# A hybrid encoder layer on one core: gates and keys made beside the input projection, and the scan's blocks in another order

## The chip, the core and the metric

The kernel runs on 1 core of one Trainium2 chip. Five engines work at the same time, each on its own queue of instructions: TensorE (PE, with its weight loads PEld), VectorE (DVE), ScalarE (ACT), GpSimd (POOL) and SyncE (SP, which here only issues DMAs). An instruction waits at the head of its queue until what it needs is there, and everything behind it waits too. The metric is the device time of one execution in microseconds (us); less is better.

## The reference

One layer of an encoder over 1024 positions of 1024 features, in float32, with one projection that feeds two mixers:

```python
proj = jnp.einsum("bsd,de->bse", h, w_in)          # h = rmsnorm(x)
glu_in, q, v, z_f, z_b, og, g_a, g_b = jnp.split(proj, SPLIT_POINTS, axis=-1)
a = jax.nn.glu(glu_in, axis=-1)
a = _dwconv_centred(a, dw_w, dw_b)                 # 31 taps, 512 channels
a = jax.nn.silu(_layernorm(a, ln_w, ln_b))
a = jnp.einsum("bsc,cd->bsd", a, pw_w)
o = _bi_hgrn2(q, v, z_f, z_b, lb[0], lb[1])        # 8 heads of 128, two directions
```

In `_bi_hgrn2` each direction turns its z into a forget gate and a key:

```python
f = lb + (1.0 - lb) * jax.nn.sigmoid(zf)
lf = jnp.log(jnp.clip(f, MIN_FORGET, 1.0))
key_gate = (1.0 - lb) * jax.nn.sigmoid(-zf)
```

and a gated linear recurrence runs over the positions with state `S_t = diag(f_t) S_{t-1} + k_t v_t^T` and output `S_t^T q_t`. Then come a norm by head times `silu(og)`, an output matrix, the merge `sigmoid(g_a) * a + sigmoid(g_b) * b`, `w_out` with the residual, a convolutional GLU feed-forward block, and a last RMSNorm.

## The kernel before

**Matmuls.** A float32 operand is split into two parts (`split`, L125: ACT rounds the high part, another engine subtracts), and `mm3` (L149 to L151) makes three matmuls of 128x128 by 128x512 for each k. TensorE gets its instructions in the order in which the program writes them; the other engines' order is set by a planner, except for instructions marked with `pin`, which keep the program's order among themselves. The work is written as streams of pieces: a piece is six such matmuls, and `Stream.fill(n)` lets n pieces be written at that place, fractions being carried over.

**Input pairs** (`pair_job`, `in_pair`). Two column tiles of `w_in` are made together by seven products in place of eight. The products run in the order 1, 2, 6, 7, 5, 4, 3, two pieces each, so a pair has 14 pieces. ACT copies three of them to SBUF pages (`su`, L440), and four evacuations (`evac`) follow, after products 2, 5, 4 and 3: three of them a DVE sum or difference of a product and an `su` page (`ev`, L800), the last straight from PSUM. 19 pairs make 38 of 56 tiles: q and og of each head, then v, z forward and z backward of each head but the last. The last head's two z tiles and the 16 tiles of g_a and g_b are made later as ordinary jobs (`rest_jobs`). The sums of weights that a pair needs are made by accumulating DMAs from GpSimd's queue (L302), or, with `first`, by DVE (L298): so for pair 0 and pairs 14 to 18. `store` (L796 to L806) evacuates a tile to an `ev` page (three of them) and stores it to DRAM through SP's queue; z is stored raw.

**Convolution and norm beside the pairs.** The 124 steps of the depthwise convolution (L1036, L1039, on DVE, four channel tiles in the pages `gl`) are written between pieces of pairs, `CONV_FILL` = 1.67 pieces a step. Then comes the LayerNorm of two halves: load, mean by a matmul with ones (L1065), squares, a reciprocal root (two small GpSimd operations, L592 and L593, then four ACT copies and a matmul, L600 and L601), and for each of four channel tiles two DVE operations, Silu on ACT (L1079), a split and two stores. The fills there are 6, 6 and 5 pieces, and 12 (`LN_LAST`) after all four tiles.

**The scan** (L1150 to L1480). 16 blocks: 8 heads by two halves of 512 positions. For block i the inputs are loaded (`scan_inputs`: q, both z; ACT makes two sigmoids and f of each z, L1163 to L1165; DVE clamps f, L1166), two blocks ahead. `scan_base` then works in five steps: it scales the keys (L1224), and doubles the span of keys `kG` and queries `qF` from 1 to 32 by DVE products (L1144), with woven copies on ACT (L1176); step 3 issues a level of 128 small matmuls (128x32, L1195, into a bank `sc`). `scan_levels` issues, with a break after each: the levels 8 and 16 (64 matmuls, L1195, into `ob`); the zeroing of a bank by 16 matmuls (`none`, L1302), the 32 blocks of span 32 (L1281) and the doubling by 32; the 16 blocks of span 64 (L1281, shape 128x64) and the doubling by 64. Four transposes of v (L1470) come after the second of these breaks has begun. `scan_states` transposes the keys (L1320), breaks, multiplies them with v (L1329), and breaks. In each of the five breaks a block writes 1.77 pieces (`FILL`) of dense jobs, one step of the next block's base, and one step of the outputs (`scan_outputs`) of the head before. Of the outputs, two steps hold 22 matmuls each (L1370) and two hold four transposes each (L1396).

**The end.** The last product of the feed-forward block runs in three parts (512, 256 and 256 positions). Each result is added (L1879) and, four pieces later, turned by transposes (`turn_out`, L1890), squared on ACT (L1892), multiplied by the final gain (L1905) and scaled by the row's factor (`scale_out`: DVE for 640 columns, L1928, ACT for the rest, L1926).

Of the kernel before, what the change touches and what calls it, by code (L numbers as in the profile page):

```python
# [15 lines left out]
ALU = mybir.AluOpType  # L16
# [4 lines left out]
TAIL = ((1, 2), (1, 1), (2, 4), (2, 3))  # L21
CONV_FILL = 1.67
NPAIRS = 19
LN_FILL = 6
LN_LAST = 12
GLU_FIRST = 4
# [3 lines left out]
GLU_LATE = 17  # L30
BASE_STEPS = 1
ALIGN = 128
# [16 lines left out]
def tile_hybrid_encoder(  # L49
# [45 lines left out]
    def nm(s):  # L95
        uid[0] += 1
        return f"{s}_{uid[0]}"
# [58 lines left out]

    chores = []

# [4 lines left out]
    def advance_chores(n=1):  # L163
        for c in list(chores):
            c[0] -= n
            if c[0] <= 0:
                chores.remove(c)
                c[1]()

    class Weights:  # L170
# [393 lines left out]
    d_og = scratch("d_og", NH, 2)  # L564
    d_z = scratch("d_z", 2, NH, 2)
    d_bm = scratch("d_bm", NH, 2)
# [229 lines left out]
    def store(dst, func=None):  # L796
# [11 lines left out]
        return evac  # L808

    todo = [  # L810
        t
# [5 lines left out]
    ]  # L817
    todo += [
        t
        for h in range(NH)  # L820
        for t in (
            (OFF_V + h * DK, store(d_v[h])),
            (OFF_ZF + h * DK, store(d_z[0][h])),
            (OFF_ZB + h * DK, store(d_z[1][h])),
        )
    ]
    todo += [(OFF_GA + i * P, store(d_ga[i], AF.Sigmoid)) for i in range(ND)]
    todo += [(OFF_GB + i * P, store(d_gb[i], AF.Sigmoid)) for i in range(ND)]

    def in_pair(n):  # L830
        (c0, e0), (c1, e1) = todo[2 * n], todo[2 * n + 1]
        evs = (e0, e1)
        return pair_job(
            in_cols(c0),
            in_cols(c1),
            NK2,
            lambda i: ht[i],
            p1,
            p1,
            lambda e, *quadrant: evs[e](*quadrant),  # L840
            first=n == 0 or n >= 14,
            columns=2,
        )
# [145 lines left out]
    V.tensor_scalar(lbw[:, 3, :], lbw[:, 2, :], -1.0, 1.0, op0=ALU.mult, op1=ALU.add)  # L989

    def lb_of(d, h):
        return lbw[:, 2, d * NH + h : d * NH + h + 1]
# [63 lines left out]
    for half in range(2):  # L1056
        xs = []
        for j in range(NCW):
            if j % 2 == 0:
                both = p1.tile([P, 2, H], F32, tag="ca", name=nm("cx"), bufs=2)  # L1060
            nc.sync.dma_start(both[:, j % 2, :], d_cv[j][half])
            xs.append(both[:, j % 2, :])
        s_pairs.fill(LN_FILL)
        mean = bank("ob")
        T.matmul(mean, ones_m, total(xs, tmp()), start=True, stop=True)  # L1065
        for t in xs:
            V.scalar_tensor_tensor(t, mean, -1.0 / CW, t, op0=ALU.mult, op1=ALU.add)
# [7 lines left out]
        rs = next(rstd)  # L1075
        for j, xn in enumerate(xs):
# [68 lines left out]

    kscale = cp.tile([P, 2 * NH], F32, name="kscale")
    V.tensor_scalar(kscale, lbw[:, 3, :], DK**-0.5, None, op0=ALU.mult)

    def c4(t):
        return t.rearrange("p (c t) -> p c t", c=4)  # L1150

    def scan_inputs(i):
# [7 lines left out]
        for d in range(2):  # L1160
            z = page(hp, "zi", 3)
            nc.sync.dma_start(z, d_z[d][h][half])
            A.activation(kG[:, d, :], z, AF.Sigmoid, scale=-1.0)  # L1163
            A.activation(z, z, AF.Sigmoid)
            A.activation(f[:, d, :], z, AF.Identity, scale=oml_of(d, h), bias=lb_of(d, h))  # L1165
        V.tensor_scalar(f, f, MIN_FORGET, 1.0, op0=ALU.max, op1=ALU.min)  # L1166
        return q, f, kG, kscale[:, h : h + NH + 1 : NH]

# [48 lines left out]
    def scan_base(ins):  # L1217


        q, f, kG, ks = ins  # L1220
        qF = hp.tile([P, 2, H], F32, tag="qF", name=nm("qF"), bufs=4)
        D_t = hp.tile([P, 4, 32], F32, tag="D", name=nm("D"), bufs=3)
        for d in range(2):
            V.tensor_scalar(kG[:, d, :], kG[:, d, :], ks[:, d : d + 1], None, op0=ALU.mult)  # L1224
        k_d, Q1 = page(hp, "A", 8), page(hp, "A", 8)
# [44 lines left out]
    def scan_levels(base, S_t, Tt):  # L1270
# [24 lines left out]
        level(slot(b, 0), A8, row(Q8))  # L1295
        level(slot(b, 1), A16, row(Q16))
        for n, m in enumerate((m_8, m_16)):
            V.copy_predicated(D_t, over(m), near(slot(b, n)))
        yield
        b = bank("sc")  # L1300
        for at, g, _ in each():
            T.matmul(b[g, at : at + 32], none, none, start=True, stop=True)  # L1302
# [137 lines left out]
    cur = Base(scan_inputs(0))  # L1440
    ins = scan_inputs(1)
    dense.fill(7)
    for pieces in (3, 4, 4, 3, 0):
        cur.step(1)
        dense.fill(pieces)
    pending = Stream(iter(()))
    for h in range(NH):
# [4 lines left out]
        for half in range(2):  # L1452
            i = 2 * h + half
            base = cur.result()
            ahead = Base(ins) if i + 1 < NI else None
            ins = scan_inputs(i + 2) if i + 2 < NI else None

            def between(fill):
                dense.fill(fill)
                if ahead is not None:  # L1460
                    ahead.step(BASE_STEPS)
                pending.fill(1)

            S_t = hp.tile([P, 4, P], F32, tag="S", name=nm("S"), bufs=3)
            vl = load(d_v[h][half])
            for n, _ in enumerate(scan_levels(base, S_t, Tt[:, half])):
                if n == 1:
# [4 lines left out]
                    A.copy(v.rearrange("p c e -> p (c e)"), b)  # L1472
                between(FILL)
            qF, kG = base[:2]
            for _ in scan_states(i, kG, v, Tt, Sf, Sb):
                between(FILL)
            kept.append((S_t, v, qF))
            cur = ahead
        pending = Stream(outputs(h, kept, Tt, Sf, Sb))
# [560 lines left out]
```

## Time and profile before

| | us |
|---|---|
| median of 3 runs | 1736.81 |
| lowest and highest run | 1735.74 and 1737.69 |
| the profiled execution's own time | 1736.41 |
| its span, from the first to the last instruction | 1734.3 |
| DMA moved | 308.27 MB, mean 178 GB/s |

The mean granted TensorE clock was 0.998. The profile counts an engine as busy from the start of an instruction to its end. Matmuls overlap, so PE's busy time says little about how densely it runs; the distance from one start to the next, or the number of matmuls in a stretch, does. In rows of groups the last field is the engine's idle time just before them and what ended it. In rows of waits the three numbers are the total in us, the count and the longest.

### The profile page before, as it was taken

The page shows a single profiled execution, that of the slowest core. Times are in us where ns is not written, and L with a number is a line of the kernel's source. Part 1 is how long each engine was busy: PE and PEld are TensorE (multiplying, and loading weights), DVE is VectorE, ACT ScalarE, POOL GpSimd, SP SyncE. Part 2 cuts the span into 40 slices and gives each one's busy share as a digit, 9 for nine tenths or more (in the row PEclk, how much of TensorE's full clock was granted, in tenths as well). Part 3 has the DMA queues.
Part 4 walks back from the last instruction along what each step waited for, and adds up shares of the span by engine and source line. Part 5 has one row for each costly group of instructions (what it writes and reads, how often), then busy time and mean ns, then how long its engine had stood idle before and what let it go on. Part 6 is the DMA issues. An engine that isn't in the chain of part 4 may idle for free.

```text
span 1734.3 us, 30669 instructions
## 1 busy us (share of the span) xinstructions
PE 1709.2 (99%) x11902; PEld 1415.0 (82%) x11902; DVE 1255.9 (72%) x1937; ACT 830.3 (48%) x1544; POOL 170.4 (10%) x185
## 2 busy tenths in 40 slices
PE   8999999999999999999999999999999999999997
PEld 6878888888788888888878888888888888888787
DVE  5599999746778888888557466667767776657865
ACT  7444443334566777776442245444434433542334
POOL 2211111100000000000000002011111111000110
PEclk9999999999999999999999999999999999999999
DMA  8768888854673444435579466568777776783842
GB/s 288 239 167 184 193 194 193 197 167 154 207 230 104 131 126 132 127 115 192 175 248 333 147 207 205 146 148 170 158 170 160 180 172 153 229 267 107 205 91 98
DMA packets 343751, 308.27 MB, mean 178 GB/s; under 512 B 25262, under 2 KB 255798, under 8 KB 343606
## 3 DMA queue, kind: packets, MB, share of 16 engines
q1 hardware_dynamic: 289590, 267.51, 48.7%
q0 software_dynamic: 44800, 37.76, 15.2%
q10 hardware_dynamic: 9216, 1.05, 0.4%
q8 instruction: 93, 1.52, 0.4%
q14 instruction: 52, 0.43, 0.1%
HBM read 201.40 MB, written 87.03 MB: 166 GB/s over the span
## 4 chain that ended last, share of the span: by engine, by line
PE 44%; DMA 2%; DVE 2%; ACT 1%; issue 1%; SPq 0%; POOL 0%; POOLq 0%; ACTq 0%; DVEq 0%
PE mm L151 10%; PE mm L150 10%; PE mm L149 10%; PE sc L149 3%; PE sc L150 3%; PE sc L151 3%; PE tr L149 1%; PE tr L150 1%; PE tr L151 1%; DMA tm<-d_bm 1%; DVE hx L125 0%; DMA wr<-in_ffn_w_down_dram 0%; DMA wr<-wr 0%; DMA d_gc<-ft 0%; DVE wp L125 0%
## 5 line engine op out<-in xcount | busy, mean ns | idle before, releaser
L149 PE MATMUL mm<-hx,wp 128*128 128x512 f32 x1068 | 428.0, 401 | 3.3 <-ACT tm L851 2.1
L151 PE MATMUL mm<-hx,wp 128*128 128x512 f32 x1068 | 418.1, 391 | 0.9 <-DVE wp L125 0.8
L150 PE MATMUL mm<-hx,wp 128*128 128x512 f32 x1068 | 416.9, 390 | 0.3 <-DVE hx L125 0.2
L125 ACT CAST wp<-wr 128x1024 fp32r<-128x1024 f32 (+2 forms) x147 | 147.2, 1002 | 259.2 <-PE mm L150 119.5
L151 PEld LDWEIGHTS mm<-hx,wp 128*128 128x128 f32 x1068 | 200.9, 188 | 46.3 <-DVE wp L125 3.4
L149 PEld LDWEIGHTS mm<-hx,wp 128*128 128x128 f32 x1068 | 200.8, 188 | 46.1 <-ACT tm L851 2.6
L150 PEld LDWEIGHTS mm<-hx,wp 128*128 128x128 f32 x1068 | 201.2, 188 | 41.3 <-DVE hx L125 1.6
L125 DVE TENSOR_TENSOR wp<-wr,wp 128x1024 fp32r<-128x1024 f32 (+2 forms) x145 | 169.3, 1168 | 68.5 <-ACT wp L125 67.9
L1039 DVE SCALAR_TENSOR_TENSOR acc<-gl,v_b,acc 128x1024 f32<-128x1024 f32 x120 | 148.9, 1277 | 0.4
L1144 DVE TENSOR_TENSOR qF<-qF,tb 128x512 f32<-128x512 f32 x96 | 65.0, 684 | 20.8 <-ACT A L1176 20.7
L440 ACT COPY su<-mm 128x512 f32<-128x512 f32 x82 | 47.7, 582 | 66.2 <-PE mm L151 66.2
L149 PE MATMUL tr<-hx,wp 128*128 128x512 f32 x180 | 70.5, 392 | 0.0
L125 ACT CAST wq<-sw 128x1024 fp32r<-128x1024 f32 x41 | 43.2, 1053 | 56.3 <-PE mm L150 40.5
L151 PE MATMUL tr<-hx,wp 128*128 128x512 f32 x180 | 70.1, 389 | 0.0
L150 PE MATMUL tr<-hx,wp 128*128 128x512 f32 x180 | 70.0, 389 | 0.0
L1636 DVE SCALAR_TENSOR_TENSOR tm<-gp,v_a,tm 128x512 f32<-128x512 f32 x88 | 65.9, 749 | 3.9 <-ACT tm L1634 2.0
L1144 DVE TENSOR_TENSOR kG<-kG,tb 128x512 f32<-128x512 f32 x96 | 65.1, 684 | 3.7 <-PE sc L1281 3.7
L149 PE MATMUL mm<-hy,wp 128*128 128x512 f32 x164 | 64.2, 391 | 0.0
L149 PE MATMUL sc<-hy,wq 128*128 128x512 f32 x164 | 64.2, 391 | 0.0
L151 PE MATMUL sc<-hy,wq 128*128 128x512 f32 x164 | 63.8, 389 | 0.0
L150 PE MATMUL mm<-hy,wp 128*128 128x512 f32 x164 | 63.8, 389 | 0.0
L150 PE MATMUL sc<-hy,wq 128*128 128x512 f32 x164 | 63.8, 389 | 0.0
(372 smaller groups left out, 3609.9 us busy)
## 6 DMA issues: line engine op xcount, KB each, us to landing
wr<-in_w_in_dram SPq DMA_DIRECT2D x48, 512.0 KB
wr<-in_ffn_w_up_dram SPq DMA_DIRECT2D x22, 512.0 KB
sw<-in_w_in_dram SPq DMA_DIRECT2D x38, 256.0 KB
d_g<-ft SPq DMA_DIRECT2D x38, 256.0 KB
sw<-in_ffn_w_up_dram SPq DMA_DIRECT2D x38, 256.0 KB
sw<-in_ffn_w_up_dram POOLq DMA_DIRECT2D x19, 512.0 KB, 8.1
wr<-sw POOLq DMA_DIRECT2D x32, 256.0 KB, 3.8
wr<-wr POOLq DMA_DIRECT2D x32, 256.0 KB, 4.1
```

Of the source, the lines that this page charges most:

```text
L125: parts = A.copy(hi, src), eng.tensor_tensor(lo, src, hi.bitcast(F32), op=ALU.subtract)
L149: T.matmul(acc, whi[:, k, :], ahi, start=first, stop=False, skip_group_check=again)
L150: T.matmul(acc, whi[:, k, :], alo, start=False, stop=False, skip_group_check=again)
L151: T.matmul(acc, wlo[:, k, :], ahi, start=False, stop=last, skip_group_check=again)
L440: A.copy(t, acc)
L1039: V.scalar_tensor_tensor(acc, g[:, k : k + S], tap(k), acc, op0=ALU.mult, op1=ALU.add)
L1144: V.tensor_tensor(o, a, b, op=op)
L1636: V.scalar_tensor_tensor(c, g[:, o + k : o + k + H], vec("fdw", k * NF + j), c, op0=ALU.mult, op1=ALU.add,)
```

## The change

Three things. **Gates and keys:** `store_gates` replaces the raw store of z. At each of the next three pieces one step runs: the complement's sigmoid into a key page (`complement`), the gate's sigmoid and the key's scale (`forget`), the affine bound (`bound`); two pieces later the clamp. Gate and key are stored through GpSimd's queue. The tiles are dealt in another order (q and og, six v, gates of heads 0 to 6, the last two v), and pairs 12 and 13 too make their weight sums on DVE. The scan loads gates and keys ready made. **Norm:** Silu becomes a sigmoid on ACT and a product on DVE, with 1.5 pieces between the two and after each tile; other fills are 9 for the first, and 1.6 for a step of the convolution. **Scan and end:** levels 8 and 16, zeroing and the 32-blocks are one group with no break between them; a break with only v's transposes follows; then the 64-blocks. The first step of a base moves to the last break of the block before last, and in a break the outputs' step comes ahead of the base's. At the end, parts of 256 turn out six pieces late and scalings are six pieces apart.

```diff
-CONV_FILL = 1.67
+CONV_FILL = 1.6
-LN_LAST = 12
+LN_STEP = 1.5
-BASE_STEPS = 1
...
+    chores, paced = [], collections.deque()
...
     def advance_chores(n=1):
...
+        if paced:
+            paced.popleft()()
...
+    def gl_page():
+        return gp0.tile([P, 2, H], F32, tag="gl", name=nm("kp"), bufs=NCW)[:, 0, :]
+
+    def store_gates(d, h, key_page):
+        def evac(half, x0, x1=None, op=None):
+            f, x, key = ev(), x0, []
+            if x1 is not None:
+                V.tensor_tensor(f, x0, x1, op=op)
+                x = f
+
+            def complement():
+                key.append(key_page())
+                pin(A.activation(key[0], x, AF.Sigmoid, scale=-1.0))
+
+            def forget():
+                pin(A.activation(f, x, AF.Sigmoid))
+                if h == 0:
+                    pin(A.activation(key[0], key[0], AF.Copy, scale=kscale_of(d, h)))
+                else:
+                    pin(V.tensor_scalar(key[0], key[0], kscale_of(d, h), None, op0=ALU.mult))
+
+            def bound():
+                pin(A.activation(f, f, AF.Identity, scale=oml_of(d, h), bias=lb_of(d, h)))
+                later(1, lambda: G.dma_start(d_k[d][h][half], key[0]))
+                later(2, clamp)
+
+            def clamp():
+                eng = G if h == 0 else V
+                pin(eng.tensor_scalar(f, f, MIN_FORGET, 1.0, op0=ALU.max, op1=ALU.min))
+                later(1, lambda: G.dma_start(d_f[d][h][half], f))
+
+            paced.extend((complement, forget, bound))
+
+        return evac
...
-    todo += [
-        t
+    values = [(OFF_V + h * DK, store(d_v[h])) for h in range(NH)]
+    gate_tiles = [
+        (off + h * DK, store_gates(d, h, gl_page if 0 < h < NPAIRS - 12 else tmp))
         for h in range(NH)
-        for t in (
-            (OFF_V + h * DK, store(d_v[h])),
-            (OFF_ZF + h * DK, store(d_z[0][h])),
-            (OFF_ZB + h * DK, store(d_z[1][h])),
-        )
+        for d, off in enumerate((OFF_ZF, OFF_ZB))
     ]
+    n = 2 * (NPAIRS - 12)
+    todo += values[:-2] + gate_tiles[:n] + values[-2:] + gate_tiles[n:]
...
-            first=n == 0 or n >= 14,
+            first=n == 0 or n >= 12,
...
-        s_pairs.fill(LN_FILL)
+        s_pairs.fill(LN_FILL + 3)
...
-            A.activation(xn, xn, AF.Silu)
-            both = gp0.tile([P, 2, H], F32R, tag="gl", name=nm("ch"), bufs=NCW)
-            for dst, part in zip(d_ca[j][half], split(both[:, 0, :], both[:, 1, :], xn, V)):
-                nc.sync.dma_start(dst, part.bitcast(F32))
-        s_pairs.fill(LN_LAST)
+            sig = tmp()
+            A.activation(sig, xn, AF.Sigmoid)
+            s_pairs.fill(LN_STEP)
+            V.tensor_tensor(xn, xn, sig, op=ALU.mult)
+            store_parts(j)
+            s_pairs.fill(LN_STEP)
...
         for d in range(2):
-            z = page(hp, "zi", 3)
-            nc.sync.dma_start(z, d_z[d][h][half])
-            A.activation(kG[:, d, :], z, AF.Sigmoid, scale=-1.0)
-            A.activation(z, z, AF.Sigmoid)
-            A.activation(f[:, d, :], z, AF.Identity, scale=oml_of(d, h), bias=lb_of(d, h))
-        V.tensor_scalar(f, f, MIN_FORGET, 1.0, op0=ALU.max, op1=ALU.min)
-        return q, f, kG, kscale[:, h : h + NH + 1 : NH]
+            nc.sync.dma_start(f[:, d, :], d_f[d][h][half])
+            nc.sync.dma_start(kG[:, d, :], d_k[d][h][half])
+        return q, f, kG
...
-        for d in range(2):
-            V.tensor_scalar(kG[:, d, :], kG[:, d, :], ks[:, d : d + 1], None, op0=ALU.mult)
...
         level(slot(b, 1), A16, row(Q16))
+        S_b = bank("sc")
+        for at, g, _ in each():
+            T.matmul(S_b[g, at : at + 32], none, none, start=True, stop=True)
+        blocks(S_b, 32)
         for n, m in enumerate((m_8, m_16)):
             V.copy_predicated(D_t, over(m), near(slot(b, n)))
-        yield
-        b = bank("sc")
-        for at, g, _ in each():
-            T.matmul(b[g, at : at + 32], none, none, start=True, stop=True)
-        blocks(b, 32)
         tb = double(tb, 32)
         yield
+        yield
+        b = S_b
         blocks(b, 64)
...
-    ins = scan_inputs(1)
+    ahead = Base(scan_inputs(1))
...
+    ahead.step(1)
...
-            def between(fill):
-                dense.fill(fill)
-                if ahead is not None:
-                    ahead.step(BASE_STEPS)
+            following = Base(scan_inputs(i + 2)) if i + 2 < NI else None
+
+            def between(n):
+                dense.fill(FILL)
                 pending.fill(1)
+                step_of = ahead if n < 4 else following
+                if step_of is not None:
+                    step_of.step(1)
...
-            cur = ahead
+            cur, ahead = ahead, following
...
-        later(4, lambda: turn_out(i, half, chunks))
+        later(8 - len(chunks), lambda: turn_out(i, half, chunks))
...
-        st.fill(4 * ND * (n + 1) + 3 - st.count)
-        finish(*part, late=2 + 2 * n)
+        st.fill(4 * ND * (n + 1) + (3, 5)[n] - st.count)
+        finish(*part, late=6)
```

`store_parts` is the split and the two stores that stood in the loop; `kscale` is now made ahead of the pairs.

More of the change, by code (lines that the diff above doesn't have):

```diff
@@ L153, in tile_hybrid_encoder @@
     PRODUCTS = (1, 2, 6, 7, 5, 4, 3)
-    chores = []
+    chores, paced = [], collections.deque()
     def later(n, do):
@@ L564, in tile_hybrid_encoder @@
     d_og = scratch("d_og", NH, 2)
-    d_z = scratch("d_z", 2, NH, 2)
+    d_f = scratch("d_f", 2, NH, 2)
+    d_k = scratch("d_k", 2, NH, 2)
     d_bm = scratch("d_bm", NH, 2)
@@ L989, in tile_hybrid_encoder, with kscale_of @@
     V.tensor_scalar(lbw[:, 3, :], lbw[:, 2, :], -1.0, 1.0, op0=ALU.mult, op1=ALU.add)
+    kscale = cp.tile([P, 2 * NH], F32, name="kscale")
+    V.tensor_scalar(kscale, lbw[:, 3, :], DK**-0.5, None, op0=ALU.mult)
+    def kscale_of(d, h):
+        return kscale[:, d * NH + h : d * NH + h + 1]
     def lb_of(d, h):
@@ L1075, in tile_hybrid_encoder, with store_parts @@
         rs = next(rstd)
+        def store_parts(j):
+            both = gp0.tile([P, 2, H], F32R, tag="gl", name=nm("ch"), bufs=NCW)
+            for dst, part in zip(d_ca[j][half], split(both[:, 0, :], both[:, 1, :], xs[j], V)):
+                nc.sync.dma_start(dst, part.bitcast(F32))
         for j, xn in enumerate(xs):
@@ L1144, in tt @@
         V.tensor_tensor(o, a, b, op=op)
-    kscale = cp.tile([P, 2 * NH], F32, name="kscale")
-    V.tensor_scalar(kscale, lbw[:, 3, :], DK**-0.5, None, op0=ALU.mult)
     def c4(t):
@@ L1217, in scan_base @@
     def scan_base(ins):
-        q, f, kG, ks = ins
+        q, f, kG = ins
         qF = hp.tile([P, 2, H], F32, tag="qF", name=nm("qF"), bufs=4)
         D_t = hp.tile([P, 4, 32], F32, tag="D", name=nm("D"), bufs=3)
-        for d in range(2):
-            V.tensor_scalar(kG[:, d, :], kG[:, d, :], ks[:, d : d + 1], None, op0=ALU.mult)
         k_d, Q1 = page(hp, "A", 8), page(hp, "A", 8)
@@ L1454, in tile_hybrid_encoder @@
             base = cur.result()
-            ahead = Base(ins) if i + 1 < NI else None
-            ins = scan_inputs(i + 2) if i + 2 < NI else None
-            def between(fill):
-                dense.fill(fill)
-                if ahead is not None:
-                    ahead.step(BASE_STEPS)
+            following = Base(scan_inputs(i + 2)) if i + 2 < NI else None
+            def between(n):
+                dense.fill(FILL)
                 pending.fill(1)
+                step_of = ahead if n < 4 else following
+                if step_of is not None:
+                    step_of.step(1)
             S_t = hp.tile([P, 4, P], F32, tag="S", name=nm("S"), bufs=3)
@@ L1472, in tile_hybrid_encoder @@
                     A.copy(v.rearrange("p c e -> p (c e)"), b)
-                between(FILL)
+                between(n)
             qF, kG = base[:2]
-            for _ in scan_states(i, kG, v, Tt, Sf, Sb):
-                between(FILL)
+            for n, _ in enumerate(scan_states(i, kG, v, Tt, Sf, Sb)):
+                between(3 + n)
             kept.append((S_t, v, qF))
-            cur = ahead
+            cur, ahead = ahead, following
         pending = Stream(outputs(h, kept, Tt, Sf, Sb))
```

## The prediction

> **What bounds the kernel now.** I read the busy shares first, then busy time by stretch, then who ended PE's waits.
>
> ```profile
> span 1734.3 us, 30669 instructions
> PE 1709.2 (99%) x11902; PEld 1415.0 (82%) x11902; DVE 1255.9 (72%) x1937; ACT 830.3 (48%) x1544; POOL 170.4 (10%) x185
> ```
>
> TensorE is the bound, and the change adds or removes no matmul: the same 38 column tiles go through pairs, the same 18 after them, and the scan issues the same blocks. So time moves only where PE waits, or where it streams slower than it could. The stretches (busy time of PE, PEld, DVE, ACT, POOL; clock; DMA share; GB/s) say how much that is:
>
> ```profile
> 150.00:200.00 50.00, 50.00 (x222) 41.41 (x221) 49.91 (x49) 20.56 (x30) 8.50 (x8) 1.00 0.89 202
> 390.00:409.00 19.00, 19.00 (x84) 15.38 (x83) 9.59 (x12) 5.52 (x9) 0.00 (x0) 1.00 0.48 149
> 409.00:430.00 21.00, 21.00 (x97) 17.12 (x96) 13.29 (x20) 9.25 (x17) 1.23 (x2) 1.00 0.44 135
> 430.00:450.00 20.00, 19.26 (x85) 15.61 (x84) 15.38 (x22) 10.40 (x17) 0.00 (x0) 1.00 0.87 289
> 450.00:470.00 20.00, 20.00 (x90) 15.97 (x89) 13.69 (x20) 9.77 (x17) 2.15 (x2) 1.00 0.27 85
> 500.00:875.00 375.00, 372.59 (x5885) 313.46 (x5884) 297.24 (x651) 258.83 (x584) 12.87 (x14) 1.00 0.45 140
> ```
>
> In the first row 222 matmuls of 512 columns fill 50 us: one starts every 0.225 us, and there is nothing to win. (The conv taps fill DVE there, but PE does not wait for them.) The norm sits in 390 to 470 us, the scan in the last row. The larger ones of PE's waits that the change can reach, each with its total, its times and its longest:
>
> ```profile
> PE sc L1281 <- DVE qF L1144: 2.0, 2, 1.0
> PE sc L1890 <- ACT y L1926: 1.5, 1, 1.5
> PE mm L149 <- DVE ev L800: 0.8, 1, 0.8
> PE mm L149 <- ACT su L440: 0.7, 1, 0.7
> ```
>
> That is 5.0 us, the ceiling for stalls. Anything more must come from how PE streams.
>
> **The scan's blocks regrouped.** PE's order is written by hand, so the new neighbours are certain. PE's timeline (start, length, group) shows what a switch between wide and narrow matmuls costs:
>
> ```profile
> 622.02 0.39 PE L151 MATMUL mm<-hx,wp 128*128 128x512 f32 x1
> 622.34 0.76 PE L1195 MATMUL ob<-A,A 128*32 128x32 f32 x64
> 623.03 0.50 PE L149 MATMUL mm<-hx,wp 128*128 128x512 f32 x1
> 623.36 0.39 PE L150 MATMUL mm<-hx,wp 128*128 128x512 f32 x1
> ...
> 625.99 0.28 PE L1302 MATMUL sc<-none 128*32 128x32 bf16 x16
> 626.10 0.47 PE L1281 MATMUL sc<-qF,kG 128*32 128x32 f32 x32
> ```
>
> Going in: 622.34 - 622.02 = 0.32 us, 0.09 over the usual 0.23. Coming out: from the 64 level products to the next wide start 0.69 us pass. By the other level, below, 32 products take 610.42 - 610.15 = 0.27 us, so 64 take 0.54, and up to 0.15 is the way out; I count 0.13. (The first wide matmul after a group takes 0.33, 0.10 too long; after a 128x128 group that happens too, so it stays out of the sum.)
>
> ```profile
> 606.23 0.39 PE L1370 MATMUL ob<-Sb,qF 128*128 128x128 f32 x2
> 606.55 0.69 PE L1281 MATMUL sc<-qF,kG 128*64 128x64 f32 x16
> ...
> 610.15 0.46 PE L1195 MATMUL sc<-q,A 128*32 128x32 f32 x32
> 610.42 1.18 PE L1195 MATMUL sc<-A,A 128*32 128x32 f32 x96
> 611.57 0.46 PE L1370 MATMUL ob<-v,S 128*128 128x128 f32 x2
> ...
> 617.50 0.39 PE L151 MATMUL mm<-hx,wp 128*128 128x512 f32 x1
> 617.73 1.05 PE L1329 MATMUL sc<-v,kT 128*128 128x128 f32 x8
> 618.62 1.06 PE L1329 MATMUL mm<-v,kT 128*128 128x128 f32 x8
> 619.43 0.48 PE L149 MATMUL mm<-hx,wp 128*128 128x512 f32 x1
> ```
>
> Groups of 128x128 pay nothing: in at 0.23 after the wide one, eight in 0.89, and the last eight, with the way out, in 0.81. So the four transposes of v, which now stand alone, cost their work only.
>
> First merge: level 8 and 16, zeroing and 32-blocks become one group. Gone are one way in (0.09) and one way out (0.13): 0.22 us, 16 times, **-3.5 us**.
>
> Second merge: the 64-blocks follow the first level (128 products) at once. Gone are that level's way in (0.09) and its way out to the next group (0.13 again): 0.22. What the step from 128*32 to 128*64 costs no row shows. It lies between 0 (as from the zeroing into the 32-blocks: 16 in 0.11 us and no gap) and a full way out, 0.13. The nearest row is another change of shape, 606.55 - 606.23 less two matmuls of 0.11 = 0.10, and I take that: 0.12 times 16, **-1.9 us**, ends -1.4 and -3.5.
>
> The Trainium skill, TensorEngine Tiling (Array Packing), Key Properties, says that changing the tiling mode drains the TensorE, and that a change of tile within a mode does not; it gives no figure. The rows above agree. By that rule the second merge puts a drain of its own between 32- and 64-wide blocks and is worth its lower end, 1.4.
>
> The 2.0 us that L1281 waits for qF arise where the 64-blocks come one fill after the 32-blocks, while DVE still doubles qF by 32. Now two fills and a level lie between: **-2.0 us**.
>
> What is late next: the doubling by 64, whose keys PE transposes (L1320). Until now a fill, the level of 1.4 us and the outputs' steps covered it; the level is gone from there. A fill is 1.77 pieces of six matmuls, 2.4 us; against it stand one doubling of keys and whatever DVE has ahead. Bounds: 0, and one doubling, 0.68 us, at each of 16 blocks: 11 us. DVE is less busy in the scan than before (below), so I take **+1.0**.
>
> **Gates and keys.** Groups of instructions (count, busy, mean ns, idle before), and one transfer with its time to landing:
>
> ```profile
> L1163 ACT ACTIVATE kG<-zi 128x512 f32<-128x512 f32 x32 | 19.5, 635 | 0.1
> L1165 ACT ACTIVATE f<-zi,lbw 128x512 f32<-128x512 f32 x32 | 25.6, 815 | 0.0
> L440 ACT COPY su<-mm 128x512 f32<-128x512 f32 x82 | 47.7, 582 | 66.2 <-PE mm L151 66.2
> L1224 DVE TENSOR_SCALAR kG<-kG,kscale 128x512 f32<-128x512 f32 x32 | 15.3, 481 | 17.6 <-ACT kG L1163 17.5
> L1166 DVE TENSOR_SCALAR f<-f 128x1024 f32<-128x1024 f32 x16 | 11.1, 691 | 6.5 <-ACT f L1165 6.3
> L1144 DVE TENSOR_TENSOR kG<-kG,tb 128x512 f32<-128x512 f32 x96 | 65.1, 684 | 3.7 <-PE sc L1281 3.7
> L125 POOL TENSOR_TENSOR hx<-ev,hx 128x512 fp32r<-128x512 f32 x8 | 11.1, 1386 | 22.0 <-ACT hx L125 22.0
> wr<-sw POOLq DMA_DIRECT2D x32, 256.0 KB, 3.8
> ```
>
> The scan loses 32 x (0.635 + 0.635 + 0.815) = 67 us of ACT, the second sigmoid taken at the first's price, and 26 us of DVE: of 375 us ACT falls from 259 to 192, DVE from 297 to 271. That shortens nothing by itself, because PE was busy beside it; it is why I price the new wait low. SP loads two gate and two key pages a block in place of two raw ones, 8.4 MB more in 375 us: 22 GB/s on top of 140, and nobody waits for them, since they are asked for a whole block ahead.
>
> The work reappears beside the pairs. A gate pair has four evacuations: ACT gains 4 x 2.085 less a copy of 0.58, 7.8 us; DVE gains 4 x (0.48 + 0.48) = 3.8 us, a 512-wide clamp lying between half of 0.691 and 0.48. A pair lasts 14 pieces of 1.36 us, 19 us, so both fit. For the first head ACT scales (0.6) and GpSimd clamps (0 to 1.4 us, its 128x512 subtraction); only stores wait for these. The weights' sums of two pairs move from accumulating DMAs to DVE, 2.7 us each at 0.68 a page, where taps have run ahead of their place. The stores leave SP's queue for POOL's, one gate page and one key page each time in place of one raw page. There they stand behind the norm's small power operation or ahead of it; PE needs no store before the scan, and the norm's fill of five pieces covers one or two issues. Each store keeps one of three ev pages for some 8 pieces with its landing of 3.8 us, which makes DVE wait at times, but not PE.
>
> The norm's turn decides. From 390 to 470 us DVE is busy 9.59 + 13.29 + 15.38 + 13.69 = 52 us, ACT 35. To that come 3.9 gate pairs and 8 products with the sigmoid: DVE 52 + 15 + 5.5 = 72 of 80 us, ACT 35 + 30 = 65. Both fit, but each hand-over to PE (a copy su, a difference ev) meets a fuller queue. What the dealing out removes is L149's wait for su, which fell among the norm's Silus: **-0.7**. The 0.8 at L800 I leave; DVE is as full there as before. For new waits I take two or three of the size seen, **+2.0** (0 to 20, below).
>
> **The end.** The 1.5 us at L1890 came when four scalings of y met the transposes of the next part. Begun later and spaced by six pieces, they no longer meet: **-1.5**, bounds 0 and -1.5.
>
> **Sum:** -3.5 - 1.9 - 2.0 + 1.0 - 0.7 + 2.0 - 1.5 = -6.6. The profiled execution took 1736.41 us, 2.1 over its span and 0.4 under the median of 1736.81; from its own time, 1729.8 us. About 0.2%, 3.5 us, is what a measurement of this kernel can tell from no change.
>
> **The rivals.**
> 1. The crowded norm ends slower. Some 27 hand-overs from ACT or DVE to PE lie in its 4.6 pairs (three su, three ev a pair). If DVE at 72 of 80 us falls behind, each comes late by the 0.75 us seen: 18 late cost 13.5 us in place of 2, so 1729.8 + 11.5 = 1741.3 us. From 12 late ones on no gain is left. For it: ACT's gate steps are pinned in order, and DVE has 8 us of slack in 80. Against: before, with DVE at 99% in the conv, only a few came late. Chance 0.10.
> 2. The kG transposes take over the wait of the 64-blocks: half of the 11 us, 5.5 in place of 1.0, gives 1734.3 us. For it: the second half of a head has only 2.4 us and one group of transposes as cover. Against: keys come first in the doubling. Chance 0.15, counted as no difference.
> 3. Everything fits, no new waits, the 64-blocks joined for nothing: -3.5 - 3.5 - 2.0 - 0.7 - 1.5 = -11.2, 1725.2 us. Chance 0.25.
> 4. The forecast, 1726.5 to 1732.5 us: 0.50.
>
> That PE's groups do not become neighbours is no rival, because their order is fixed in the program.
>
> **How the numbers follow.** Faster 0.50 + 0.25 = 0.75; within 0.2% 0.15; slower 0.10. The range takes in cases 2 to 4 with their ends: 1723 (case 3 with the 0.8 of L800 and an unlisted short wait gone too) to 1737 (case 2 with a few late hand-overs).
>
> **What would show it.** In PE's timeline L1302 starts right after L1195's ob with no wide matmul between, and the 128*64 group of L1281 right after L1195's sc. The scan's stretch is some 6 us shorter. Among PE's waits L1281 for qF and L1890 for y are gone; a new row of L1320 for kG is the price of the shorter cover. Many short waits for ev and su between 375 and 470 us are rival 1. The forecast is wrong if merged groups keep gaps of 0.1 us, or if PE shows holes in the norm.

## The result, and the profile after

The changed kernel takes 1755.09 us (median of 4 runs, 1753.06 to 1755.94) beside 1737.25 us for the kernel before (4 runs, 1735.74 to 1739.19): ratio 1.0098, 95% interval 1.0085 to 1.0111. It is slower by 17.8 us. The prediction was 1729.8, within 1723 to 1737, with a chance of 0.10 for slower.

The busy shares of the changed kernel hide it, since PE counts as busy at half clock too:

```profile
span 1752.6 us, 30885 instructions
PE 1711.9 (98%) x11902; PEld 1422.0 (81%) x11902; DVE 1269.3 (72%) x1959; ACT 822.2 (47%) x1537; POOL 207.3 (12%) x247
```

The number of matmuls is the same. To see where the time went I use the zeroing matmuls (`none`), of which each of the scan's 16 blocks has 16, as marks. The view of one tile gives count, shortest, median and longest duration in ns, and the first and last start in us. Before, and then after:

```profile
L1302 PE MATMUL sc<-none x256: 176/176/190, 517.6 to 849.5; 128*32 128x32 bf16 x128
```

```profile
L1339 PE MATMUL sc<-none x256: 176/184/188, 543.9 to 865.0; 128*32 128x32 bf16 x128
```

From the first zeroing to the last the scan now lasts 865.0 - 543.9 = 321.1 us in place of 331.9: it **gained 10.8 us**. But it starts 26.3 us late. The regrouped block zeroes one break earlier (the experiment `scan_end`, whose pairs are those of before, has its first zeroing at 515.5, 2.1 us earlier), so the stretch beside the pairs **lost 28.4 us**. What is left, 18.3 + 10.8 - 28.4 = 0.7 us, lies behind the scan (a wait of 1.9 us for `hx` at 908 us is new there, with 3.4 us at half clock behind it).

The loss has three rows in the view of PE's waits between 100 and 545 us (total, count, longest); before, they were 0.8 for `ev` and 0.7 for `su`:

```profile
PE mm L148 <- ACT su L441: 8.8, 5, 3.9
PE ob L613 <- DVE tm L1095: 7.2, 2, 4.1
PE mm L148 <- DVE ev L802: 3.7, 2, 3.5
```

These are few and long, 19.7 us in 9 waits. Here is how three of them arise. The first is on DVE at 167 us, in the conv's stretch, where no gate has been made yet. Before (start, length, engine, line):

```profile
161.79 6.06 DVE L1039 SCALAR_TENSOR_TENSOR acc<-gl,v_b,acc 128x1024 f32<-128x1024 f32 x5
167.77 0.68 DVE L800 TENSOR_TENSOR ev<-su,mm 128x512 f32<-128x512 f32 x1
```

and after:

```profile
161.59 6.06 DVE L1081 SCALAR_TENSOR_TENSOR acc<-gl,v_b,acc 128x1024 f32<-128x1024 f32 x5
167.57 1.22 DVE L124 TENSOR_TENSOR wq<-sw,wq 128x1024 fp32r<-128x1024 f32 x1
168.71 1.28 DVE L1081 SCALAR_TENSOR_TENSOR acc<-gl,v_b,acc 128x1024 f32<-128x1024 f32 x1
169.90 0.68 DVE L124 TENSOR_TENSOR wq<-w,wq 128x512 fp32r<-128x512 f32 x1
170.50 0.68 DVE L802 TENSOR_TENSOR ev<-su,mm 128x512 f32<-128x512 f32 x1
```

The difference that frees a PSUM bank ran right behind five taps; now a weight's subtraction, one more tap and another subtraction stand ahead of it, and it starts 2.7 us later. PE waits 3.5 us for it. The second is on ACT (in brackets: idle before it and what ended that):

```profile
376.25 0.82 ACT L834 ACTIVATE ev<-ev,lbw 128x512 f32<-128x512 f32 x1
381.76 0.60 ACT L827 ACTIVATE ev<-mm 128x512 f32<-128x512 f32 x1 [4.70 <-DMA d_f<-ev]
382.26 1.04 ACT L124 CAST wp<-wr 128x1024 fp32r<-128x1024 f32 x1
383.19 0.59 ACT L441 COPY su<-mm 128x512 f32<-128x512 f32 x1
```

and PE at the same place:

```profile
380.67 0.39 PE L150 MATMUL sc<-hy,wq 128*128 128x512 f32 x1
383.83 0.50 PE L148 MATMUL mm<-hy,wq 128*128 128x512 f32 x1 [2.77 <-ACT su L441]
```

A gate's sigmoid writes a new `ev` page and finds all three taken: it waits 4.70 us for an older gate's store to land. Behind it in ACT's queue stand a cast and the copy `su`, and PE waits for that copy.

The third, PE's 3.9 us at 451 us, has the same form, but here ACT waits 3.78 us for a page of the key, whose store has not landed:

```profile
452.62 0.60 ACT L824 ACTIVATE kp<-mm 128x512 f32<-128x512 f32 x1 [3.78 <-DMA d_k<-kp]
454.82 0.58 ACT L441 COPY su<-mm 128x512 f32<-128x512 f32 x1
```

The two waits for `tm` are of another kind: these are sums of the norm's squares, and before the first of them ACT works without a break from 409.7 to 420.4 us, its four squares standing between gate steps and casts.

The waits are not all. Stretches of the changed kernel (us; busy time of PE, PEld, DVE, ACT, POOL with counts; granted clock; DMA share; GB/s):

```profile
163.60:170.40 6.80, 4.19 (x19) 3.14 (x17) 6.80 (x7) 1.68 (x2) 0.86 (x1) 1.00 0.34 73
170.50:177.20 6.70, 5.96 (x14) 4.71 (x15) 4.87 (x6) 2.12 (x3) 1.58 (x1) 0.50 0.77 207
384.00:387.40 3.40, 3.40 (x15) 2.75 (x16) 2.35 (x4) 0.97 (x2) 0.00 (x0) 1.00 0.00 0
481.10:484.40 3.30, 3.30 (x9) 2.61 (x8) 0.00 (x0) 1.75 (x5) 1.23 (x2) 0.50 0.00 0
```

From 170.4 us, late in the wait at 167 us, the **granted clock is 0.50** for 6.8 us, and likewise from 419.6 and 453.7 (6.8 us) and 481.1 (3.4 us). In 3.3 us at half clock 9 matmuls run, in 3.4 us at full clock 15. Of the matmuls in these four stretches 37 start 0.43 us behind the one before in place of 0.23: 37 x 0.2 = 7.4 us. The kernel before has one such stretch (98.8 us, 3.4 us long, 7 matmuls, 1.4 us lost). So: 19.7 - 1.5 of waits and 7.4 - 1.4 of slow matmuls make 24.2 of the 28.4 us; the rest is in gaps below the size that the waits list.

### The profile page after: what moved, and what is told of

Its sections match the earlier page's. It is cut to its first block, busy times and chain, and to the rows that moved or that the text cites. A ratio compares the mean times of both kernels' runs of the same rounds, so it can differ in the third digit from the quotient of the medians.

```text
span 1752.6 us, 30885 instructions
## 1 busy us (share of the span) xinstructions
PE 1711.9 (98%) x11902; PEld 1422.0 (81%) x11902; DVE 1269.3 (72%) x1959; ACT 822.2 (47%) x1537; POOL 207.3 (12%) x247
```

## The experiments

Every run is compared with the kernel before on its own chip (medians there 1739 to 1741), so the ratios are what to compare, and within one kernel the zeroing marks.

**The scan alone.** `scan_end`: before, with the regrouped blocks and the end's new spacing only.

> The kernel before with the regrouped scan and the new end alone; gates and keys are still made in the scan, and the norm keeps its Silu. Theory A (the scan's and the end's parts work as forecast, and the loss is all beside the pairs): PE's stretches of scan and end shrink by 8 to 10 us, so 1727 to 1730 us against some 1737 of before, and no new hole between 105 and 470 us. Rival B (the scan gains only because ACT and DVE were relieved of the gates there): 4 us or less, with new waits of PE at the first level or the 32-blocks.

1736.83 us, ratio 0.9985 (0.9972 to 0.9998). The scan from first to last zeroing takes 330.4 us, 1.5 less than before. The qF wait is gone, but PE's waits in the scan have new rows:

```profile
PE tr L1321 <- DVE kG L1144: 5.2, 3, 2.4
PE sc L1195 <- ACT A L1176: 1.8, 3, 1.4
PE sc L1330 <- ACT kT L1323: 1.2, 2, 0.8
```

That is the size of the second of the two expectations, if not its place. And it is rival 2 of the prediction: with the gates' 67 us of ACT and 26 us of DVE still in the scan, the transposes of the keys come too early for the doubling.

**The gates without the regrouping.** `gates_only`: the changed kernel with the scan's blocks grouped as before.

> The changed kernel with the scan's steps grouped as before (one block-pair bank later, inputs one block ahead): the gates are made beside the pairs, but the scan isn't regrouped. If the move of the gates shortens nothing in the scan by itself, as I predicted, the scan lasts about the 331 us that it has in the kernel before, and the kernel takes 1764 us. If the move takes away waits by itself, the scan lasts 326 us or less and the kernel takes 1757 to 1760. In either case slower than the changed kernel.

1770.07 us, ratio 1.0171 (1.0136 to 1.0207). Its marks, and PE's wait in the scan:

```profile
L1343 PE MATMUL sc<-none x256: 176/176/190, 551.3 to 882.8; 128*32 128x32 bf16 x128
```

```profile
PE sc L1322 <- DVE qF L1194: 2.4, 4, 1.0
```

The scan lasts 331.5 us: the move of the gates by itself shortens nothing there. Neither part alone gains (0.4 and 1.5 us), both together gain 10.8. (Beside the pairs it is 5 us slower than the changed kernel, its first zeroing being at 551.3, less 2.1 for the break, beside 543.9, with the same code there: the planner places DVE's and ACT's work anew for every version, and a few us of such differences are not resolved here.)

**The taps' spacing and the norm's edit, each on the kernel before.**

```diff
-CONV_FILL = 1.67      # conv_160: this line alone
+CONV_FILL = 1.6
```

> The kernel before with CONV_FILL 1.6 in place of 1.67 and nothing else. If the taps' spacing makes the loss that norm_only showed between 150 and 400 us (8 us of holes and half clock), it is here too: 1744 to 1750, holes at 167 to 170 us. If the dealt-out norm makes it, 1737 to 1740.

> The kernel before with the norm's edit alone (sigmoid and a product in place of silu, dealt out with 1.5 pieces after each, fills 9, 6, 5, CONV_FILL 1.6); gates and scan as before. If the norm's edit costs by itself, or the conv's fill of 1.6 does, it shows as holes at 167 us or between 350 and 500 us and a time of 1741 to 1746. If these only cost because the gate steps stand in the same queues, 1736 to 1738, the time before.

> The kernel before with the norm's edit (sigmoid and product, dealt out with 1.5 pieces after each), but CONV_FILL 1.67 and the first fill 6 as before. If the spacing makes the loss of norm_only, this takes the time of before, 1735 to 1740; if the dealt-out norm does, 1745 to 1750.

`conv_160`: 1748.66 us, ratio 1.0042 (1.0030 to 1.0054). `norm_only` (the norm's edit with 1.6): 1750.05, 1.0068 (1.0050 to 1.0087). `norm_167` (the norm's edit with 1.67 and the first fill 6): 1739.06, 0.9993 (0.9980 to 1.0006). So the one constant costs 0.42% alone, and at 1.67 the norm's sigmoid and product, dealt out, cost and gain nothing that can be measured. (At 1.6, with the first fill of 9, they may cost 0.26% more; the two intervals just touch.) Their rows for the wait between 120 and 400 us, `conv_160` and then `norm_167`:

```profile
PE mm L149 <- DVE ev L800: 7.4, 4, 3.5
```

```profile
PE mm L149 <- DVE ev L800: 1.4, 2, 1.1
```

and DVE's order in `conv_160`, which is that of the changed kernel, without any gate:

```profile
162.80 6.06 DVE L1039 SCALAR_TENSOR_TENSOR acc<-gl,v_b,acc 128x1024 f32<-128x1024 f32 x5
...
169.91 1.28 DVE L1039 SCALAR_TENSOR_TENSOR acc<-gl,v_b,acc 128x1024 f32<-128x1024 f32 x1
...
171.71 0.69 DVE L800 TENSOR_TENSOR ev<-su,mm 128x512 f32<-128x512 f32 x1
```

**The change with the spacing undone.** `after_167`: CONV_FILL 1.67, the norm's first fill 6, all else as changed.

> The changed kernel with CONV_FILL 1.67 and the norm's first fill 6 as before; gates, stores and scan as changed. If the spacing costs its 7 us independently of the gates, 1747 to 1749 beside the change's 1755. If the pieces that it uses up come back as holes in the norm, 1752 to 1758.

1748.13 us, ratio 1.0048 (1.0035 to 1.0061): 0.0050 less than the change's 1.0098, about what the spacing costs alone. Its first zeroing is at 535.4, 8.5 us earlier. That the number meets the first expectation is in part luck. The hole at 167 us goes, and so do all but 0.8 of the 7.2 us for the squares' sums, but with three pieces fewer ahead of the norm's mean a long wait comes there, with 13.7 us at half clock from 458.6 us on, within it and behind it:

```profile
PE ob L1107 <- DVE tm L1095: 10.0, 1, 10.0
463.14 0.43 DVE L840 TENSOR_SCALAR ev<-ev 128x512 f32<-128x512 f32 x1 [4.49 <-ACT ev L834]
```

The sum of the mean (L1095, at 463.88) stands on DVE behind that clamp of a gate; the clamp waits for ACT, and ACT had waited 1.79 us for a key's store and 2.67 us for a gate's. Two of the norm's own pages were loaded late too, at 456.4. What is left of the loss is the gates, since `norm_167` costs nothing.

**The gates' pages, queue and work, one at a time, on the change.** `f_in_key_page` keeps the gates of heads 1 to 6 in the unused half of the key's `gl` page; `stores_on_sp` moves both stores to SP's queue; `no_complement` makes the key on DVE from the gate's page, without the second sigmoid (so from the gate, not from its complement).

> The changed kernel, but for heads 1 to 6 the gate f lies in the unused half of its key's page, so that no gate holds one of the three ev pages. ACT and DVE do the same work. Theory P (pages: PE waits because ACT's and DVE's next writes into ev stand still until a store on GpSimd's queue has landed, and su copies stand behind them): the waits of ACT and DVE for the DMA of d_f, 10.5 and 8.4 us between 330 and 510 us, go, PE's holes at 380, 403 and 451 us shrink to under 1 us, and the time falls by 6 to 14 us, to some 1741 to 1749, with what the clock loses after the holes. Rival L (load: ACT and DVE are simply too full there): within 3 us of the changed kernel's 1755.

> The changed kernel with the stores of gates and keys issued by SyncE, as the raw store of z was, in place of GpSimd. Theory P: if the queue makes the hold long (a store stands behind another one that waits for its clamp), pages come free sooner and the time falls by 3 to 10 us; if SyncE's queue is itself held by weight loads that wait for pages, stores come later and the time grows. Rival L: within 3 us of 1755 either way, because the engines' work is the same.

> The changed kernel without the complement's sigmoid: the key page is made by DVE (for the first head by ACT) from the gate's page instead, so ACT has 0.62 us less for each evacuation, some 2.5 us a gate pair of 19 us, and the key is not the reference's. Pages are held as long as before. Rival L: the excess beside the pairs shrinks by a third or more, the time falls by 6 to 12 us. Theory P: the waits for d_f stay, and the time stays within 4 us of 1755.

Ratios 1.0041 (1.0024 to 1.0059), 1.0058 (1.0037 to 1.0078) and 1.0045 (1.0030 to 1.0060), times 1745.62, 1750.00 and 1748.10 us. Each takes off a part of 0.4 to 0.6%; none names a single cause (the first two go against theory L, the third against theory P). In `f_in_key_page` the hole at 380 us is gone, but PE's waits keep these rows:

```profile
PE mm L148 <- DVE ev L802: 4.1, 2, 3.6
PE ob L613 <- DVE tm L1101: 4.0, 2, 2.3
```

**Other fills.** Three tries to mend both holes by fills, of the mean, of the squares, between squares and column matmuls, and behind them.

> The changed kernel with the gates of heads 1 to 6 kept in the unused half of the key's page, and CONV_FILL back at 1.67 as in the kernel before. The first alone gave 1745.6 us. If the wait of PE at 167 us comes from the conv's taps standing 0.07 of a piece closer together (five taps, 6.06 us, then lie ahead of the evacuation's tensor_tensor on DVE), the 3.6 us hole at 167 us goes, and with it the 6.8 us at half clock that follow it (some 3 us): 1739, between 1738 and 1741. If that hole comes from the gate evacuations themselves, it stays in another place: 1744 to 1747.

> As f_and_conv_fill, and in the norm the three pieces added ahead of the mean's matmul are put behind the squares instead, with one more (fills of 6, 6, 4, 5 where the change has 9, 6, 0, 5). If the two holes of 2.3 us of the norm's column matmuls at 415 and 474 us come from squares that stand on ACT behind bunched gate steps, they go, with the half clock behind the first (some 3 us): together with the conv fill 1732 to 1736, below the kernel before. If the norm is crowded as a whole (ACT and DVE have too much in those 180 us), the holes come back at the evacuations of the next pieces and the time stays at 1738 to 1741.

> The changed kernel with the gates of heads 1 to 6 in the unused half of the key's page, CONV_FILL 1.64 and the norm's fills 6, 6, 2, 5. The version with 1.67 and 6, 6, 4, 5 ran out of pieces at the end of the norm (two holes at 502 us) and had one hole of 6 us at 455 us, ahead of the mean. If the pages are what is short, the 6 us hole stays in some form: 1736 to 1742. If the fills alone were wrong, 1730 to 1733.

`f_and_conv_fill`: 1745.28 us, ratio 1.0033 (1.0019 to 1.0046): the hole at 167 us goes, as the first expectation has it, but the time is that of the second, since a wait of 6.2 us for a gate's difference (L825) comes at 441 us. The pairs have 19 x 14 = 266 pieces; 124 steps at 1.67 and two norms of 32 ask for 271, so the last fills find none. `f_conv_norm_fill`: 1741.09, 1.0005 (0.9992 to 1.0018), with one wait of 5.9 us for the sum of the mean, from which the pieces were taken: the second expectation, a crowded norm. `f_fills_164`: 1744.05, 1.0025 (1.0003 to 1.0048), slower than either expectation. In these three a fill moves a hole at least as often as it closes one.

**No key beside the pairs.** The key is the complement of the gate, one minus f, so the scan can make it in one operation a block:

```diff
-            paced.extend((complement, forget, bound))   # and the key's page, scale and store
+            paced.extend((forget, bound))
...
+        V.tensor_scalar(kG, f, -(DK**-0.5), DK**-0.5, op0=ALU.mult, op1=ALU.add)
         k_d, Q1 = page(hp, "A", 8), page(hp, "A", 8)
```

> The changed kernel with no key made or stored beside the pairs: the key equals one minus the gate, so the scan makes it by one DVE operation a block from the gate's page (128x1024, about 0.8 us, 16 blocks). Per evacuation this takes away the complement sigmoid, the scaling, one page and one store; the gate steps are 2 in place of 3. The gates of the forward direction of heads 1 to 6 lie in the gl pages, the others in ev pages. If the loss beside the pairs comes from pages held until a store lands, with the load on ACT and DVE behind it, both are halved: the holes at 380, 417, 451 and 476 us go, the one at 167 us (the conv's fill) stays with its half clock, and the scan keeps its 321 us or loses the 12 us of DVE work that lie beside PE: 1729 to 1734, faster than before. If the loss comes from the dealt-out norm and the conv fill, it stays: 1746 to 1752.

> As key_in_scan, with CONV_FILL 1.64 and the norm's fills 6, 6, 2, 5 in place of 9, 6, 0, 5 (the two pieces in the third place stand between the squares and the column matmuls). The 167 us hole goes with its half clock (6.5 us) if the conv's spacing sets it; 1723 to 1728, the best version of all.

> key_in_scan (no key beside the pairs; the scan makes it from the gate) with CONV_FILL 1.67 and the norm's first fill 6 as before. With spacing and pages both mended only the scan's gain of 11 us and some 5 us of the norm are left: 1728 to 1732, ratio 0.994 to 0.997. If the holes move into the norm as in f_and_conv_fill, 1738 to 1741.

`key_in_scan`: 1738.08 us, ratio 0.9997 (0.9982 to 1.0012), between its two expectations. `key_conv_norm`: 1741.40, 1.0012 (0.9997 to 1.0026), a miss: with fewer pieces ahead of the mean PE waits 4.1 us there. `key_167` (CONV_FILL 1.67 and the old first fill): **1733.01 us, ratio 0.9967** (0.9950 to 0.9984), faster than both kernels. Its marks, beside those of `after_167`:

```profile
L1329 PE MATMUL sc<-none x256: 176/184/188, 523.2 to 843.9; 128*32 128x32 bf16 x128
```

```profile
L1339 PE MATMUL sc<-none x256: 176/184/188, 535.4 to 857.6; 128*32 128x32 bf16 x128
```

The scan keeps its gain (320.7 us), and the pairs give back 12.2 us. Most of that is one place: the wait for the sum of the mean is 1.6 us here, 10.0 in `after_167`.

**Which half of the key it was.** `key_ev` puts the hold of the pages back (every gate in an `ev` page, stored six pieces late), `key_load` the work (two 128x128 sigmoids and two scalings on a page that nothing stores).

> key_167 with every gate in one of the three ev pages and stored six pieces after its evacuation, as the change does it (key_167 has half of heads 1 to 6 in gl pages and stores after four pieces). No key work. If the pages held until a store has landed make the loss between after_167 and key_167 (12 us), most of it comes back: 1739 to 1745, with waits of DVE or ACT for d_f's landing of 1 to 5 us and holes of PE behind them. If the load makes it, 1731 to 1735.

> key_167 with the key's work put back beside the pairs, on a small page of its own that is never stored: two 128x128 sigmoids on ACT (some 0.64 us, as one of 512) a step ahead of the gate's, and two scalings of 128x128 on DVE. No page is held and nothing is stored for it. If load on ACT and DVE makes the 12 us, most of it comes back: 1739 to 1745. If the pages make it, 1731 to 1736.

1732.84 us, ratio 0.9959 (0.9944 to 0.9974), and 1732.93, 0.9962 (0.9947 to 0.9978): **neither brings anything back**. Each lies in the range that its expectation gives to the other cause, so neither is enough alone. `key_ev` does have the page waits; two rows of DVE and ACT between 330 and 525 us:

```profile
ACT ev L822 <- DMA d_f<-ev: 6.7, 4, 1.9
DVE ev L818 <- DMA d_f<-ev: 6.3, 1, 6.3
```

and PE's longest wait there is 2.0 us. So 13 us of page waits on the two engines were hidden where the key's work was not in the same queues, and the work was hidden where no gate's page was waited for. The loss needs both, or the key's own page and store; no run put these back by themselves, and that stays open. The traces of the changed kernel and of `after_167` point at the key's page, for which ACT waits 3.78 and 1.79 us ahead of the 3.9 and 10.0 us that PE waits; neither `key_ev` nor `key_load` has such a page.

**Holes put into PE's work.** `holes`: before, with PE made to wait six times for a chain of small GpSimd operations.

> The kernel before with six holes put into PE's work beside the pairs, at conv steps 48, 60, 72, 84, 96 and 108: a one-column matmul, a copy on ACT, 2, 5, 8, 11, 14 or 17 operations on a 128x1 page on POOL, and a second one-column matmul that waits for them. If a hole of PE costs its own length only, the time grows by the holes, some 1 to 6 us each. If the clock is halved behind holes of over about 3.3 us, as the records of the changed kernel suggest, each of the longer holes is followed by 3.4 or 6.8 us at half clock that cost another 1.5 to 3 us, and the shorter ones by none.

1794.41 us (one run), span 1792.5. PE's waits, and the stretches at half clock of two holes, of 4.0 and 7.8 us:

```profile
PE ob L1056 <- POOL hole L1055: 36.0, 6, 8.3
```

```profile
229.20:232.50 3.30, 3.30 (x9) 2.63 (x9) 0.00 (x0) 0.45 (x1) 1.62 (x1) 0.50 0.07 19
372.50:382.60 10.10, 4.81 (x12) 3.90 (x13) 0.00 (x0) 0.59 (x1) 2.62 (x9) 0.50 0.24 43
```

The first zeroing comes 572.1 - 517.6 = 54.5 us later for 36.0 us of holes: together they cost one and a half times their length. Each came with 3.4, 6.8 or 10.2 us at half clock, the shortest (3.2 us) too. Over the whole run 64 wide matmuls start 0.43 us behind the one before, 49 more than in the kernel before: 49 x 0.2 = 9.8 of the other 18.5 us. A wait of 2.2 us for a late `ev` is in them too, with 3.4 us at half clock of its own; the rest was not traced.

## Why the prediction was wrong

**What bounds the kernel** was read rightly: the number of matmuls is the same and all of the difference is PE's waits and PE's clock.

**The scan's merges** were right in mechanism; the first was priced too high, the second too low, and the sum too low. Before, the way from a wide matmul through the 32-blocks to the next group is 626.50 - 625.67:

```profile
625.67 0.39 PE L151 MATMUL mm<-hx,wp 128*128 128x512 f32 x1
...
626.50 0.66 PE L1470 MATMUL tr<-ident,tm 128*128 128x128 f32 x4
```

and after, both merged groups:

```profile
647.86 0.39 PE L150 MATMUL mm<-hx,wp 128*128 128x512 f32 x1
648.18 0.75 PE L1237 MATMUL ob<-A,A 128*32 128x32 f32 x63
...
649.34 0.50 PE L148 MATMUL mm<-hx,wp 128*128 128x512 f32 x1
...
654.86 1.07 PE L1237 MATMUL sc<-A,A 128*32 128x32 f32 x96
655.86 0.69 PE L1321 MATMUL sc<-qF,kG 128*64 128x64 f32 x16
```

First merge: 1.01 + 0.83 us with two wide matmuls (0.23 each) before, 1.48 with one after, so 0.13 a block in place of 0.22: -2.1, not -3.5. Second: the 96 products and their way on take 1.00 in place of 1.15, and the way into the 64-blocks (0.10) is gone, so 0.25 in place of 0.12: -4.0, not -1.9. The mis-sized term is the level's way out, put at 0.13 after the 64 products. The prediction's own row had more: 96 products and their way on take 1.15, three times the 0.27 of 32 is 0.81, and 0.34 is left. The step to the 64-blocks does cost something, 1.00 - 0.81 = 0.19 by the same count; the lower end of 1.4 had taken it for the whole way out. With 2.3 us of waits gone (2.0 for qF, 0.3 for kT) that makes 8.4 of the 10.8 us, if all blocks are like these; the rest was not assigned. **The new wait for kG** (+1.0) does not occur in the changed kernel, and is 5.2 us where the gates stay in the scan.

**"That shortens nothing by itself"** holds to the letter (331.5 beside 331.9 us). What it left out is that the regrouping gains only because of it: the two parts were priced one by one, and their gain is joint.

**The taps' spacing was not priced at all.** I quoted DVE at 49.91 of 50 us in the conv, noted that PE does not wait for the taps, and passed over the constant that packs them closer. Alone it is a term of +0.42%, 7 us (`conv_160`), which by itself undoes the forecast gain. In the change it does not simply add: undone with the first fill it gives back 0.50% (`after_167`), but 0.08% from `f_in_key_page` to `f_and_conv_fill`, because other holes come.

**"Which makes DVE wait at times, but not PE"** is the step of the gates that failed, and with it the **+2.0** for new waits; PE's waits there became 19.7 us in place of 1.5, 3.5 of them the taps'. DVE and ACT do wait for pages (4.70 us at 376 us for a gate's, 3.78 at 448 us for a key's), but each is one queue: what PE waits for, an `su` copy or an `ev` difference, stands behind the waiting instruction. I had named what fills the queues (DVE 72 of 80 us) and what holds the pages, and judged each to fit by its mean; each does fit, as `key_load` and `key_ev` show; with the key's own page and store beside them they do not, and which of these it needs stays open.

**The price of a hole** was wrong for every term of this kind: I priced a wait at its length, and the clock's fall adds to it. The sign of it stood in the trace of before, where the 2.3 us hole at 94.8 us is followed by 3.4 us at half clock from 98.8 us.

**The norm's su wait** (-0.7) and the end's (-1.5): both small terms are of the right kind and too small to measure alone. `norm_167` starts the scan 0.6 us earlier. At the end the wait of L1890 for `y` is gone, but the same transposes, now L1932, wait 0.7 us for a square (`oj`).

**Rival 1** had the place and the sign, a crowded norm, but not the form: 18 hand-overs late by 0.75 us each. What came is 9 waits of up to 4.1 us, from pages, from the order of the queues and from the taps, and its 1741.3 us was 14 short.

## What to carry to other kernels

Price a constant that only paces an engine that is full anyway: where DVE stood at 99%, 4% closer taps put an evacuation behind one more tap and cost 7 us alone. Where work moves into a queue that also serves the bound engine, ask what a waiting instruction has behind it; means that fit one by one say little: here page waits alone cost nothing, a fuller queue alone cost nothing, and the key with its work, page and store cost 12 us. And a large intermediate that is a simple function of another (here a key that is one minus the gate) can be better made where it is used than stored.

## What the runs showed of the hardware

After a hole in PE's stream the granted clock falls to 0.50 in stretches of 3.4 us or whole multiples of it. A hole is counted here as the distance of two matmul starts less the usual 0.23 us. In the traces of before, of the change and of the experiments, all 23 holes of over 3.0 us came with it (in 17 of them before the hole had ended), as did the six of `holes`, and 16 of 33 holes between 2.0 and 2.95 us (the 2.9 us one at 380 us in the changed kernel did not). The Trainium skill, TensorE: Matmul & The Clock Gate, Part 1, says that the clock halves after an idle window of about 3.4 us, and that this window of 3413 ns runs freely; its section on HAM oscillation gives the rule of no idle gaps over about 3.4 us. The lengths agree; as a limit the rule is too mild here, since holes of 2.0 to 2.95 us were enough in about half of the cases (470 us in `key_167`: 2.2 us, then 3.4 us at half clock).
